# Sums of the first gate and up blocks in the banks of the products, and a scheduler that counts VectorE's work on SBUF as longer beside GpSimd

## The chip, the cores and the metric

The kernel runs on one core of one Trainium2 chip. The metric is the device time of one execution in microseconds, the median of several runs. The engines are called PE (TensorE, matrix products), PEld (its weight loads), DVE (VectorE), ACT (ScalarE), POOL (GpSimd) and SP (SyncE, which issues transfers here). Matrix products write to banks of PSUM, of which this part of the kernel uses eight; everything else on the chip lies in SBUF.

## The reference

One layer of a streaming encoder over 1056 tokens (1024 of a prompt and 32 of a running stream), with D_MODEL = 1024 and D_FF = 2816:

```python
def merge_and_tail(x, o_a, o_r, gate_a, gate_r, p, w_o, g_ffn, w_ff_gate, w_ff_up,
                   w_ff_down, g_ple, w_ple, w_ple_gate):
    mix = jax.nn.sigmoid(gate_a) * o_a + jax.nn.sigmoid(gate_r) * o_r
    x = x + mix @ w_o
    h = rmsnorm(x, g_ffn)
    x = x + (jax.nn.silu(h @ w_ff_gate) * (h @ w_ff_up)) @ w_ff_down
    gate = jax.nn.sigmoid(rmsnorm(x, g_ple) @ w_ple_gate)
    return x + gate * (p @ w_ple)
```

Ahead of it stand a projection of the normed input, an attention with two softmax maps per head and a retention. All inputs are float32, and every product is made of three float16 products (high by high, high by low, low by high parts).

## The kernel before

The kernel has four stages: projection, attention and retention (to 1085 us of the trace); the product with `w_o`, the residual and the norm; the gate and up products of 22 blocks of 128 columns; the down product and the tail. The change touches the second and third, which one hand-written scheduler (class `Flow`) orders together.

**Scheduler.** Work is written as generators that yield what they need: `V(n)`, `S(n)`, `G(n)` and `M(us)` are dictionaries from an engine to a cost in microseconds, `either(...)` offers one operation to two engines, `("get", key)` and `("put", key)` take and give back one of a kind of buffer, `("wait", key)` waits for an event. `Flow.run` keeps a clock per engine. Again and again it takes the candidate with the smallest key, writes it out, and so fixes the order of each engine's instructions. The key of a step with one possible engine is its start, `max(ready, engine free)`; the key of a step that two engines could take is its start plus 0.3 times its cost there. At equal keys the priority decides. On the chip each engine then works through its instructions in this order and waits at each for its inputs; the counted times play no part there.

**The second stage.** The tokens are cut in four pieces c0 to c3 (352, 352, 176 and 176 wide). `stream_bc` makes eight products with `w_o` of each piece. `residual(c)` adds each to the residual (L1534), squares and sums (L1542 on ACT, L1545 on DVE), sums over partitions with four small products (L1553), computes the root (L1557 on DVE, a power on POOL at L1560), spreads it (L1563 on DVE, a product at L1568) and scales the eight rows (L1572). The sums over partitions and the spread root lie in one PSUM bank, `ss`, allocated once as `ssb`.

**Seven products instead of eight.** The gate and up products use a Strassen-like scheme with seven products A1, S1, A2, S2, A4, S4, S3 of combined inputs x1, t1, x3, t2, t4, x4, t3. `sums(c, k)` builds t1 to t4 and x4 of an odd piece from it and the piece before, for k from 0 to 3; each addition and subtraction goes through `either_tt` (L1480), so DVE or POOL makes it. `parts16` splits each result in its high part (ACT, L1488) and its low part (through `either_tt`, L1482). The parts of x1, x3, t1 and x4 lie in the tile `mixs`, those of t2, t3 and t4 in `tT0` for the pieces c0 and c1 (352 wide) and `tT1` for c2 and c3 (176 wide). `gu_pair(j, p)` makes the seven products of block j for the pair p of pieces, in the order above, each into one of seven banks `ps`; the order of the pairs is (0,0), (1,0), (0,1), (1,1), (2,0), (2,1), (3,0) and so on. A product has 12 matrix multiplications, three for each k.

**The weights of a block.** `load_gu(j)` loads them (tile `st`), squares and sums on ACT (L1611), adds two partial sums (DVE, `wamh`, L1615), sums over partitions with one small product in `weight_scale` (PE, L300), makes the power of two from it (DVE, `p2of` and on, `guc` at L230 first), forms four combinations on POOL (`comb_w`, L1591) and splits seven times (ACT L1583, DVE L1586). The product of L300 writes into column 511 of `ssb`, the bank that the norm uses too, whose last readers are the scalings of L1572.

`gu_sums` then adds the products up out of the banks (ACT L1721, DVE L1715 and L1730), and `gu_out` makes the gated output (L1686 to L1695).

Of the kernel before, what the change touches and what calls it, by code (L numbers as in the profile page):

```python
# [21 lines left out]
P = 128  # L22
# [37 lines left out]
    return {"V": 0.07 + x + f * n / 960.0}  # L60


def S(n, x=0.0):
    return {"S": 0.1 + x + n / 1200.0}

# [11 lines left out]


def either(*ds):
    out = {}  # L80
    for d in ds:
        out.update(d)
    return out


class Flow:
# [65 lines left out]
    def run(self):  # L152
        while self.ready:
            best = None
            for c in self.ready:
                for e, us in c[4].items():
                    start = max(c[3], self.free[e])
                    k = (start + 0.0 if len(c[4]) == 1 else start + 0.3 * us, c[1], c[2])
                    if best is None or k < best[0]:
                        best = (k, c, e, start, us)  # L160
            _, c, e, start, us = best
            self.ready.remove(c)
            self.free[e] = start + us
            c[3] = start + us + (0.0 if e == "M" else LAT)
            self._step(c, e)
        assert not self.sleepers and not any(self.waiting.values())
# [17 lines left out]
def kernel(  # L184
# [104 lines left out]
    def weight_scale(amax, n, gi, tag, pool=True, norm=False, total=False, at_bank=None):  # L289


        p2 = sm(n, tag + "p2", 3)
        if total:
            if at_bank is None:
                yield ("wait", "id")
            key, psum = at_bank or ("o", ps_o)
            yield ("get", key)
            yield M(0.06)
            ps = psum[:, 511:512] if at_bank else psum.tile([P, 512], F32, tag=key, name="mt")[:, 0:1]
            nc.tensor.matmul(out=ps, lhsT=ones16, rhs=amax, start=True, stop=True)  # L300
            yield ("delay", 0.3 if at_bank else 0.0)
            yield from p2of(p2, ps, n, tag, norm)
            yield ("put", key)
        elif pool:
            yield G(0, 0.1)
            ar = sm(n, tag + "ar", 3)
            nc.gpsimd.partition_all_reduce(ar, amax, P, ABSMAX)
            yield from p2of(p2, ar, n, tag)
        else:
            ar = yield from spread_max(amax, n, tag, at_bank)  # L310
            yield from p2of(p2, ar, n, tag, norm)
            yield ("put", at_bank[0] if at_bank else "o")
        yield V(n)
        s = sm(n, tag + "s", 3)
        nc.vector.reciprocal(s, p2)
        yield V(n, 2.0)
        nc.vector.tensor_scalar(out=s, in0=s, scalar1=_f(2.0 ** (-52 if gi == 1 else -50)) if norm else 16384.0,
                                scalar2=None, op0=ALU.mult)
        d = sm(n, tag + "d", 6)
        if gi is None:  # L320
            nc.vector.tensor_scalar(out=d, in0=p2, scalar1=_f(2.0 ** (50 if norm else -14)), scalar2=None, op0=ALU.mult)
        else:
            nc.vector.tensor_scalar(out=d, in0=p2, scalar1=gd[:, gi:gi + 1], scalar2=_f(2.0 ** 64) if norm else 1.0,
                                    op0=ALU.mult, op1=ALU.mult)
        return s, d
# [1117 lines left out]
    with ExitStack() as pc:  # L1443
# [18 lines left out]
        with ExitStack() as pw:  # L1462
# [6 lines left out]

            mixs = xh1 = tail["mixs"]  # L1470
            xfs, gus, dns, banks, done = [], {}, {}, {}, []
            ssb = pss.tile([P, 512], F32, tag="ss", name="ss")

            def span(c):
                return slice(START[c], START[c] + WIDTH[c])
# [2 lines left out]
                return psb.tile([P, 512], F32, tag="ps", name="ps")[:, 0:WIDTH[c]]  # L1478

            def either_tt(n, out, in0, in1, op):  # L1480
                g = yield either(V(n), G(n))
                ENG[g].tensor_tensor(out=out, in0=in0, in1=in1, op=op)  # L1482


# [36 lines left out]
            def residual(c):  # L1521

                p, odd = divmod(c, 2)
                CW = WIDTH[c]
                cs = span(c)
                xf = xc.tile([P, KD, CW], F32, tag="xf%d" % p, name="xf", bufs=2)
                nc.sync.dma_start(out=xf, in_=xT[:, :, cs])
                xfs.append(xf)
                yield ("get", "acc")
                acc = wkb.tile([P, CH], F32, tag="acc", name="acc")[:, 0:CW]  # L1530
                for m in range(KD):
                    yield ("wait", ("wo", c, m))
                    yield V(CW, 1.0, 0.08)
                    nc.vector.scalar_tensor_tensor(out=xf[:, m], in0=banks[c, m], scalar=wos[m // 4][1][m % 4 // 2], in1=xf[:, m],  # L1534
                                                   op0=ALU.mult, op1=ALU.add)
                    yield ("put", "ps")
                    nc.sync.dma_start(out=x1_d[m, :, cs], in_=xf[:, m])
                    if m:
                        yield ("get", "sq")
                    yield S(CW, 0.05)  # L1540
                    sq = wkb.tile([P, CH], F32, tag="sq", name="sq")[:, 0:CW] if m else acc
                    nc.scalar.activation(sq, xf[:, m], AF.Square)  # L1542
                    if m:
                        yield V(CW)
                        nc.vector.tensor_tensor(out=acc, in0=acc, in1=sq, op=ALU.add)  # L1545
                        yield ("put", "sq")
                yield ("get", "ss")
                yield ("delay", 2.0 if c + 1 < NW else 0.5)
                yield M(0.3)
                B = CW // 4  # L1550
                ps = ssb
                for b in range(4):
                    nc.tensor.matmul(out=ps[0:B, CW + b:CW + b + 1], lhsT=acc[:, b * B:(b + 1) * B], rhs=ones32[:, 0:1],  # L1553
                                     start=True, stop=True)
                yield V(4, 1.0, 0.1)
                v = sm(4, "nbv")
                nc.vector.tensor_scalar(out=v[0:B], in0=ps[0:B, CW:CW + 4], scalar1=_f(1.0 / D), scalar2=EPS, op0=ALU.mult, op1=ALU.add)  # L1557
                yield G(4, 0.2)
                r = sm(4, "nbr")
                nc.gpsimd.tensor_tensor(out=r[0:B], in0=v[0:B], in1=neghalf[0:B], op=ALU.pow)  # L1560
                yield V(CW)
                dg = wkb.tile([P, CH], F32, tag="dg", name="dg")[:, 0:CW]
                nc.vector.tensor_tensor(out=dg[0:B].rearrange("p (b c) -> p b c", b=4),  # L1563
                                        in0=id32[0:B, 0:B].unsqueeze(1).broadcast_to([B, 4, B]),
                                        in1=r[0:B].unsqueeze(2).broadcast_to([B, 4, B]), op=ALU.mult)
                yield ("delay", 2.0 if c + 1 < NW else 0.5)
                yield M(0.5)
                nc.tensor.matmul(out=ps[:, 0:CW], lhsT=ones32[0:B], rhs=dg[0:B], start=True, stop=True)  # L1568
                yield ("put", "acc")
                for k in (0, 4, 1, 5, 2, 6, 3, 7):  # L1570
                    yield V(CW, 1.0, 0.08)
                    nc.vector.scalar_tensor_tensor(out=xf[:, k], in0=xf[:, k], scalar=gS[:, 1, k:k + 1], in1=ps[:, 0:CW],  # L1572
                                                   op0=ALU.mult, op1=ALU.mult)
                    if not odd:
                        flow.add(parts16((p, "x1" if k < HK else "x3", k % HK), (xh1[:, k, 0, cs], xh1[:, k, 1, cs]), xf[:, k]))
                    elif k >= HK:
                        flow.add(sums(c, k - HK))
                yield ("put", "ss")


            def split(j, w, s, i, src):
                yield S(HK * P, 0.18)
                nc.scalar.activation(w[:, i, 0], src, AF.Copy, scale=s)  # L1583
                yield ("delay", 0.4)
                yield V(HK * P, 1.0, 0.06)
                nc.vector.scalar_tensor_tensor(out=w[:, i, 1], in0=src, scalar=s, in1=w[:, i, 0], op0=ALU.mult, op1=ALU.subtract)  # L1586
                yield ("set", ("gw", j, i))

# [5 lines left out]
            def load_gu(j):  # L1594
# [19 lines left out]
                am = sm(1, "wamh", 3, BF16)  # L1614
                nc.vector.tensor_tensor(out=am, in0=am2[:, 0:1], in1=am2[:, 1:2], op=ALU.add)  # L1615
                yield ("delay", 1.5)
                s, d = yield from weight_scale(am, 1, 1, "gu", norm=True, total=True, at_bank=("sw", ssb))

                yield V(1, 1.0, 0.2)
                nc.vector.tensor_scalar(out=rf[:, j:j + 1], in0=d, scalar1=_f(2.0 ** 38), scalar2=d, op0=ALU.mult, op1=ALU.mult)  # L1620
# [21 lines left out]
            def load_dn(m):  # L1642
# [22 lines left out]
                yield V(2)  # L1665
                am = sm(1, "wamh", 3, BF16)
                nc.vector.tensor_tensor(out=am, in0=ams[:, 0:1], in1=ams[:, 1:2], op=ALU.add)
                s, d = yield from weight_scale(am, 1, None, "dn", norm=True, total=True, at_bank=("sw", ssb))
                for st, js in sts:
                    yield S(half * P, 0.18)  # L1670
                    nc.scalar.activation(w[:, 0, js], st, AF.Copy, scale=s)
# [155 lines left out]
                                halves[m, c] = bank()  # L1827
                            down_mm(halves[m, c], dns[m][0], js, c, js[0] < 16, False)

            flow = Flow(dict(ps=7, ss=1, sw=1, w=3, st=2, pr=2, th=2, acc=2, sq=2))  # L1830
            del flow.buffers["w"][1:], flow.buffers["st"][1:]
            with tc.manual_schedule(engines={mybir.EngineType.PE, mybir.EngineType.DVE, mybir.EngineType.Activation,
                                             mybir.EngineType.Pool}):
# [207 lines left out]
```

## Time and profile before

| | |
|---|---|
| median of 3 runs | 1947.84 us (1945.46 to 1948.18) |
| the profiled execution | 1947.6 us, its span 1945.8 us |
| granted clock of PE, mean | 0.994 of full |
| HBM, read and written | 113.61 MB and 31.34 MB, 74 GB/s over the span |

The table's second row is the time that the steps below are set against: the span and 1.8 us around it. The views used are the busy time by stretch, PE's waits, the instructions in order of time, and the groups by line. A bracket at the end of a row of the timeline tells how long the engine sat idle ahead of it and what ended that. A record's length contains some overlap with the next one, since instructions of an engine are pipelined; from start to start is the pace.

### The profile page before, as it was taken

The numbers are of one execution on the slowest core, as the hardware profiler recorded it, in microseconds if no ns is written. First come the engines' busy times: TensorE is split into PE (matmuls) and PEld (weight loads), VectorE is DVE, ScalarE is ACT, GpSimd is POOL, SyncE is SP. The second block draws the span as 40 slices with busy tenths as digits, with TensorE's granted clock in tenths as the row PEclk, the third lists the DMA queues.
The fourth block names the chain that finished last, engine by engine and source line by source line (L and its number), as shares of the span: only waits on it lengthen the run. The fifth ranks groups of instructions, "written<-read, shape, count | busy, mean of one in ns | idle before, by whom it ended". The sixth has DMA issues, their size and how long they took to land.

```text
span 1945.8 us, 38415 instructions
## 1 busy us (share of the span) xinstructions
PE 1885.6 (97%) x14267; PEld 1216.2 (63%) x14267; DVE 1531.5 (79%) x3995; ACT 1065.3 (55%) x2775; POOL 697.0 (36%) x1142
## 2 busy tenths in 40 slices
PE   5899999999999999999999998899999999999999
PEld 2465565555655555556556685777777776666665
DVE  7887878788878788878888579999999986753364
ACT  6676767666666666666665346555555552111132
POOL 3754444344454444444543048323223210000010
PEclk9899999999999999999999999999999999999999
DMA  5221202112121121120213721122211107211031
GB/s 194 72 72 53 83 20 72 56 49 63 33 76 59 28 79 41 52 81 18 75 57 127 268 71 34 72 94 81 74 66 45 66 31 261 78 60 61 28 131 49
DMA packets 71949, 147.44 MB, mean 76 GB/s; under 512 B 25265, under 2 KB 52017, under 8 KB 63825
## 3 DMA queue, kind: packets, MB, share of 16 engines
q1 hardware_dynamic: 71760, 144.98, 22.3%
q8 instruction: 112, 1.84, 0.4%
q14 instruction: 77, 0.62, 0.1%
HBM read 113.61 MB, written 31.34 MB: 74 GB/s over the span
## 4 chain that ended last, share of the span: by engine, by line
PE 83%; DVE 10%; ACT 2%; POOL 2%; issue 2%; DMA 1%; SPq 0%; DVEq 0%; POOLq 0%; ACTq 0%
PE pj L723 10%; PE pj L725 9%; PE pj L724 9%; PE ps L471 9%; PE ps L473 9%; PE ps L472 9%; PE ps L1458 4%; PE ps L1456 4%; PE ps L1457 4%; PE t L907 2%; PE sc L860 2%; PE sc L863 1%; PE pj L734 1%; PE t L1055 1%; PE po L926 1%
## 5 line engine op out<-in xcount | busy, mean ns | idle before, releaser
L723 PE MATMUL pj<-w,xh 128*128 128x512 f16 x1024 | 390.6, 381 | 0.7 <-ACT w L462 0.7
L724 PE MATMUL pj<-w,xh 128*128 128x512 f16 x1024 | 389.8, 381 | 1.4 <-DVE w L464 1.4
L725 PE MATMUL pj<-w,xh 128*128 128x512 f16 x1024 | 389.8, 381 | 0.0
L471 PE MATMUL ps<-mixs,w 128*128 128x352 f16 (+1 forms) x960 | 260.6, 277 | 1.5 <-DVE pws L1336 1.5
L472 PE MATMUL ps<-mixs,w 128*128 128x352 f16 (+1 forms) x960 | 260.5, 276 | 0.3 <-POOL mixs L1482 0.3
L473 PE MATMUL ps<-mixs,w 128*128 128x352 f16 (+1 forms) x960 | 260.4, 276 | 0.0
L471 PEld LDWEIGHTS <-w 128*128 128x128 f16 x1728 | 169.7, 98 | 65.6 <-issue 7.0
L473 PEld LDWEIGHTS <-w 128*128 128x128 f16 x1728 | 169.4, 98 | 55.1 <-issue 4.2
L472 PEld LDWEIGHTS <-w 128*128 128x128 f16 x1728 | 169.5, 98 | 49.6 <-issue 0.8
L725 PEld LDWEIGHTS <-xh 128*128 128x128 f16 x1024 | 100.5, 98 | 124.3 <-DVE xh L708 2.5
L1591 POOL TENSOR_TENSOR st<-st 128x512 f32<-128x512 f32 x66 | 85.9, 1301 | 251.5 <-DVE w L1586 187.0
L723 PEld LDWEIGHTS <-xh 128*128 128x128 f16 x1024 | 101.3, 99 | 77.5 <-issue 1.1
L878 ACT ACTIVATE p<-sc,nb,scs 128x256 f32<-128x256 f32 (+7 forms) x128 | 106.1, 830 | 77.6 <-DVE nb L872 29.9
L472 PE MATMUL ps<-tT,w 128*128 128x352 f16 (+1 forms) x528 | 143.6, 277 | 3.6 <-DVE tT L1482 3.6
L724 PEld LDWEIGHTS <-xh 128*128 128x128 f16 x1024 | 100.5, 98 | 72.7 <-issue 0.8
L473 PE MATMUL ps<-tT,w 128*128 128x352 f16 (+1 forms) x528 | 143.7, 277 | 0.0
L471 PE MATMUL ps<-tT,w 128*128 128x352 f16 (+1 forms) x528 | 143.6, 277 | 0.0
L1586 DVE SCALAR_TENSOR_TENSOR w<-st,gus,w 128x512 f16<-128x512 f32 x132 | 140.4, 1064 | 0.1
L870 DVE TENSOR_REDUCE nm<-sc 128x1 f32<-128x768 f32 (+6 forms) x112 | 102.5, 916 | 27.0 <-PE sc L863 25.5
L1458 PE MATMUL ps<-a,w 128*128 128x352 f16 x312 | 97.5, 313 | 0.5 <-DVE w L1677 0.5
L1457 PE MATMUL ps<-a,w 128*128 128x352 f16 x312 | 97.5, 313 | 0.0
L1456 PE MATMUL ps<-a,w 128*128 128x352 f16 x312 | 97.5, 312 | 0.0
(433 smaller groups left out, 4890.0 us busy)
## 6 DMA issues: line engine op xcount, KB each, us to landing
st<-in_win_dram SPq DMA_DIRECT2D x30, 1024.0 KB, 4.9
st<-in_wgu_dram SPq DMA_DIRECT2D x22, 1024.0 KB, 4.9
st<-in_wdn_dram SPq DMA_DIRECT2D x16, 704.0 KB, 4.5
out_dram<-kv SPq DMA_DIRECT2D x64, 128.0 KB, 1.7
a_d<-a SPq DMA_DIRECT2D x9, 528.0 KB, 2.6
b<-a_d SPq DMA_DIRECT2D x9, 528.0 KB, 8.5
mixs<-mix_d SPq DMA_DIRECT2D x8, 528.0 KB, 6.2
pw_d<-pws SPq DMA_DIRECT2D x12, 352.0 KB, 5.6
```

Of the source, the lines that this page charges most:

```text
L471: nc.tensor.matmul(out=ps, lhsT=wh, rhs=ah, start=first, stop=False)
L472: nc.tensor.matmul(out=ps, lhsT=wh, rhs=al, start=False, stop=False)
L473: nc.tensor.matmul(out=ps, lhsT=wl, rhs=ah, start=False, stop=last)
L723: nc.tensor.matmul(out=ps, lhsT=xhi, rhs=w[:, k, 0], start=(k == 0), stop=False)
L724: nc.tensor.matmul(out=ps, lhsT=xhi, rhs=w[:, k, 1], start=False, stop=False)
L725: nc.tensor.matmul(out=ps, lhsT=xh[:, k, 1, t0:t0 + P], rhs=w[:, k, 0], start=False, stop=(k == KD - 1))
L870: nc.vector.tensor_reduce(out=nm[0:R, mc], in_=pv, axis=AX.X, op=ALU.max, negate=True)
L878: nc.scalar.activation(pt[0:R, 0:NK], ps[0:R, p0:p0 + NK], AF.Exp, bias=nb[0:R, m:m + 1], scale=sc_ap[0:R], accum_out=Z[0:R, m:m + 1])
L1456: nc.tensor.matmul(out=ps, lhsT=wt[:, 0, j], rhs=a[:, 0, cs], start=(first and j == js[0]), stop=False)
L1457: nc.tensor.matmul(out=ps, lhsT=wt[:, 1, j], rhs=a[:, 0, cs], start=False, stop=False)
L1458: nc.tensor.matmul(out=ps, lhsT=wt[:, 2, j], rhs=a[:, 1, cs], start=False, stop=(last and j == js[-1]))
L1586: nc.vector.scalar_tensor_tensor(out=w[:, i, 1], in0=src, scalar=s, in1=w[:, i, 0], op0=ALU.mult, op1=ALU.subtract)
```

## The change

Three things are altered. First, `V` work that lies in SBUF alone in these stages (the additions of `either_tt`, the sums of squares, the spread root, the splits) is marked as `Shared`, and the scheduler adds to its counted cost on DVE up to 0.9 of it, as far as POOL is still taken by the scheduler's own clock. Second, the sums of `weight_scale` get a bank of their own: for blocks 0 to 3 the next of the seven banks `ps`, for the later ones and the down blocks a new tile in the bank `ss`. Third, the norm takes a new tile of that bank for each piece, and the buffer kind `sw` is gone. What is computed is the same.

```diff
+class Shared(dict):
+    pass
+
+def VS(n, f=1.0, x=0.0):
+    return Shared(V(n, f, x))
...
 def either(*ds):
-    out = {}
+    out = type(ds[0])()
...
                 for e, us in c[4].items():
                     start = max(c[3], self.free[e])
+                    if e == "V" and isinstance(c[4], Shared):
+                        us += 0.9 * min(us, max(0.0, self.free["G"] - start))
                     k = (start + 0.0 if len(c[4]) == 1 else start + 0.3 * us, c[1], c[2])
...
-            ps = psum[:, 511:512] if at_bank else psum.tile([P, 512], F32, tag=key, name="mt")[:, 0:1]
+            ps = psum.tile([P, 512], F32, tag=key, name="mt")[:, 0:1]
             nc.tensor.matmul(out=ps, lhsT=ones16, rhs=amax, start=True, stop=True)
...
-            ssb = pss.tile([P, 512], F32, tag="ss", name="ss")
...
-                g = yield either(V(n), G(n))
+                g = yield either(VS(n), G(n))
...
-                        yield V(CW)
+                        yield VS(CW)
                         nc.vector.tensor_tensor(out=acc, in0=acc, in1=sq, op=ALU.add)
...
-                ps = ssb
+                ps = pss.tile([P, 512], F32, tag="ss", name="ss")
...
-                yield V(HK * P, 1.0, 0.06)
+                yield VS(HK * P, 1.0, 0.06)
...
-                s, d = yield from weight_scale(am, 1, 1, "gu", norm=True, total=True, at_bank=("sw", ssb))
+                s, d = yield from weight_scale(am, 1, 1, "gu", norm=True, total=True, at_bank=("ps", psb) if j < 4 else ("ss", pss))
...
-                s, d = yield from weight_scale(am, 1, None, "dn", norm=True, total=True, at_bank=("sw", ssb))
+                s, d = yield from weight_scale(am, 1, None, "dn", norm=True, total=True, at_bank=("ss", pss))
...
-            flow = Flow(dict(ps=7, ss=1, sw=1, w=3, st=2, pr=2, th=2, acc=2, sq=2))
+            flow = Flow(dict(ps=7, ss=1, w=3, st=2, pr=2, th=2, acc=2, sq=2))
```

The order of the instructions changes from the norm of c1 on, on all engines. Lines behind the edits stand nine further down (L1482 is L1491 in the new file, L1591 is L1600).

POOL's queue, before, where the low parts of the first pair end and the combinations of block 1 begin. `tT0_16839` takes low parts of t2, t3 and t4 of c0 and c1 (from `xf_16850`, the rows of c0, and `xf_16853`, those of c1), `w_17827` and `st_17103` belong to block 1:

```order
L1482 TENSOR_TENSOR tT0_16839<-xf_16850,tT0_16839 128x352
L1482 TENSOR_TENSOR mixs_16401<-xf_17104,mixs_16401 128x176 x2
L1482 TENSOR_TENSOR tT0_16839<-xf_16853,tT0_16839 128x352
L1482 TENSOR_TENSOR tT0_16839<-xf_16850,tT0_16839 128x352
L1591 TENSOR_TENSOR w_17827<-st_17103 128x512
L1560 TENSOR_TENSOR nbr_18093<-nbv_18090,neghalf_68 44x4
L1591 TENSOR_TENSOR st_17103<-st_17103 128x4x128 x3
```

The same queue now, where its last three low parts for `tT0_16839` stand. `st_17675` belongs to block 2, `xf_17103` and `xf_17416` are the rows of c2 and c3, `xf_16849` and `xf_16852` those of c0 and c1 (t4 of k = 2, t2 of k = 3 and t4 of k = 3, in this order):

```order
L1491 TENSOR_TENSOR xf_17103<-xf_17416,xf_17103 128x176
L1600 TENSOR_TENSOR st_17675<-st_17675 128x4x128
L1491 TENSOR_TENSOR tT1_16840<-xf_17103,tT1_16840 128x176
L1491 TENSOR_TENSOR tT1_16840<-xf_17416,tT1_16840 128x176
L1600 TENSOR_TENSOR st_17675<-st_17675 128x4x128
L1491 TENSOR_TENSOR mixs_16401<-xf_17103,mixs_16401 128x176
L1491 TENSOR_TENSOR tT1_16840<-xf_16849,tT1_16840 128x176
L1491 TENSOR_TENSOR mixs_16401<-xf_17416,mixs_16401 128x176
L1491 TENSOR_TENSOR tT0_16839<-xf_16849,tT0_16839 128x352
L1491 TENSOR_TENSOR tT0_16839<-xf_16852,tT0_16839 128x352
L1491 TENSOR_TENSOR tT0_16839<-xf_16849,tT0_16839 128x352
```

What moved: the last low parts of the first pair stood ahead of all combinations of block 1 (one of them on DVE); now three of them stand behind all four combinations of blocks 1 and 2 each, and behind most sums of the pieces c2 and c3.

PE's queue before, at the sum over partitions of c3 (L1553) and at the spread root of c3 (L1568). The rows on `mixs` and `tT_16839` are products of the pair (0,0):

```order
L473 LDWEIGHTS w
L473 MATMUL ps<-mixs,w 128x352
L1553 MATMUL ss<-cst_sb,acc 44x1 x4
L471 LDWEIGHTS w
L471 MATMUL ps<-mixs,w 128x352
```

```order
L473 LDWEIGHTS w
L473 MATMUL ps<-tT_16839,w 128x352
L1568 MATMUL ss<-dg,cst_sb 128x176
L471 LDWEIGHTS w
L471 MATMUL ps<-tT_16839,w 128x352
```

The same place now, with the sum of block 2 (L310, into a bank of its own) behind it:

```order
L482 MATMUL ps<-mixs,w 128x352
L483 LDWEIGHTS w
L483 MATMUL ps<-mixs,w 128x352
L1562 MATMUL ss<-cst_sb,acc 44x1 x4
L1577 MATMUL ss<-dg,cst_sb 128x176
L310 LDWEIGHTS cst_sb
L310 MATMUL mt<-wamh,cst_sb 128x1
L481 LDWEIGHTS w
L481 MATMUL ps<-tT_16839,w 128x352
```

What moved: before, the products A2 and S2 (24 matrix multiplications) stood between the two steps of the norm of c3; now nothing does, and S2 with t2 stands behind both and behind the sum of block 2. The sum of block 1, which stood ahead of the first product of the pair (0,0), stands behind it.

More of the change, by code (lines that the diff above doesn't have):

```diff
@@ L1560, in residual @@
                 nc.gpsimd.tensor_tensor(out=r[0:B], in0=v[0:B], in1=neghalf[0:B], op=ALU.pow)
-                yield V(CW)
+                yield VS(CW)
                 dg = wkb.tile([P, CH], F32, tag="dg", name="dg")[:, 0:CW]
```

## The prediction

> **What bounds the kernel now.** First the span, then busy time by stretch: the columns behind the length are busy us (with the number of instructions) of PE, PEld, DVE, ACT and POOL, then PE's granted clock, the DMA share and GB/s.
>
> ```profile
> span 1945.8 us, 38415 instructions
> 1158.00:1268.00 110.00, 93.77 (x858) 73.44 (x856) 108.14 (x224) 62.90 (x146) 67.53 (x69) 0.95 0.16 55
> 1268.00:1608.00 340.00, 340.00 (x3038) 262.51 (x3036) 326.23 (x732) 195.95 (x404) 90.32 (x66) 1.00 0.19 65
> ```
>
> From 1268 us PE never rests for 340 us: what this change does there can gain nothing, unless it takes a matrix multiplication away, and it takes none. Between 1158 and 1268 us PE is idle for 16 us while DVE is busy for 108.14 of 110. That is the place the change works on: the end of the norm, the sums of the last pieces and the weights of the first blocks, all on DVE and POOL. Next, PE's waits from 1085 to 1640 us (total, times, longest), and the rows of PE's timeline at them:
>
> ```profile
> PE ss L300 <- DVE xf L1572: 8.4, 2, 6.3
> PE ps L472 <- DVE tT L1482: 3.6, 1, 3.6
> PE ss L300 <- DVE wamh L1615: 3.3, 2, 2.4
> PE ss L1568 <- DVE dg L1563: 0.4, 1, 0.4
> ```
> ```profile
> 1184.06 0.16 PE L300 MATMUL ss<-wamh,cst_sb 128*128 128x1 bf16 x1 [6.31 <-DVE xf L1572]
> 1184.09 0.45 PE L471 MATMUL ps<-mixs,w 128*128 128x352 f16 x1
> ...
> 1191.30 0.31 PE L471 MATMUL ps<-tT,w 128*128 128x352 f16 x1
> 1191.45 0.31 PE L472 MATMUL ps<-tT,w 128*128 128x352 f16 x1
> ...
> 1195.33 0.31 PE L473 MATMUL ps<-tT,w 128*128 128x352 f16 x1
> 1197.75 0.16 PE L300 MATMUL ss<-wamh,cst_sb 128*128 128x1 bf16 x1 [2.11 <-DVE xf L1572]
> ...
> 1221.63 0.31 PE L472 MATMUL ps<-tT,w 128*128 128x176 f16 x1 [3.60 <-DVE tT L1482]
> ...
> 1232.91 0.16 PE L300 MATMUL ss<-wamh,cst_sb 128*128 128x1 bf16 x1 [2.39 <-DVE wamh L1615]
> ...
> 1267.61 0.16 PE L300 MATMUL ss<-wamh,cst_sb 128*128 128x1 bf16 x1 [0.94 <-DVE wamh L1615]
> ```
>
> So in the pair (0,0) PE waits for block sums (L300), twice because these write into the bank whose last reader, a scaling of the norm (L1572), isn't through; the products with t2 (the first `tT` rows, from 1191.30 us) start without a wait.
>
> **The change part by part.** *The banks.* With banks of their own, the sums of blocks 1 and 2 no longer wait for the scalings: of 6.31 and 2.11 us those parts can go that were due to the bank. What is late next is `wamh`, which stands in DVE's queue in the middle of the same scalings (by the profile it was made 3.3 us ahead of the product at 1184.06 us):
>
> ```profile
> 1180.63 0.14 DVE L1615 TENSOR_TENSOR wamh<-gam 128x1 bf16<-128x1 f32 x1
> ```
>
> So 1 to 4 us could be gained at the first, as far as PE then has nothing worse to wait for.
>
> *The order on POOL.* It has something worse. In POOL's new queue the last three low parts of the first pair, t4 of k = 2, t2 of k = 3 and t4 of k = 3, stand behind the four combinations of block 1, the four of block 2 and most sums of c2 and c3. PE's product S2 of the pair (0,0) takes t2, k = 3 included, and its second matrix multiplication of k = 3 reads that low part; everything else of PE is queued behind. The time R at which POOL has it done is therefore a floor for PE. POOL's groups from 1158.5 to 1221.5 us, before:
>
> ```profile
> L1482 POOL TENSOR_TENSOR xf<-xf 128x352 f32<-128x352 f32 x10 | 10.0, 1001 | 8.2 <-DVE xf L1572 5.5 <-DVE xf L1482 2.6
> L1591 POOL TENSOR_TENSOR st<-st 128x512 f32<-128x512 f32 x6 | 9.0, 1507 | 1.2 <-DVE w L1586 1.0
> L1482 POOL TENSOR_TENSOR xf<-xf 128x176 f32<-128x176 f32 x12 | 8.4, 718 | 1.7 <-DVE xf L1572 0.8 <-DVE gup L234 0.8
> L1482 POOL TENSOR_TENSOR mixs<-xf,mixs 128x352 f16<-128x352 f32 x7 | 7.3, 1051 | 0.5 <-ACT mixs L1488 0.5
> L1482 POOL TENSOR_TENSOR mixs<-xf,mixs 128x176 f16<-128x176 f32 x9 | 6.2, 687 | 0.3 <-ACT mixs L1488 0.3
> L1482 POOL TENSOR_TENSOR tT<-xf,tT 128x176 f16<-128x176 f32 x7 | 5.0, 712 | 0.0
> L1482 POOL TENSOR_TENSOR tT<-xf,tT 128x352 f16<-128x352 f32 x4 | 4.1, 1045 | 0.0
> L1560 POOL TENSOR_TENSOR nbr<-nbv,neghalf 44x4 f32<-44x4 f32 x2 | 2.7, 1370 | 2.2 <-DVE nbv L1557 2.2
> L1591 POOL TENSOR_TENSOR w<-st 128x512 f32<-128x512 f32 x2 | 2.7, 1362 | 0.0
> ```
>
> The 21 wide additions took 21.4 us, 1.02 each; the 28 narrow ones 19.6, 0.70 each; the eight combinations 11.7; the two powers 2.7. The first group's 8.2 us of idle holds the 5.5 ahead of the first row; behind that POOL waited for 2.7 + 1.2 + 1.7 + 0.5 + 0.3 + 2.2 = 8.6 us. In the new queue, from its first addition to t2's last low part, stand 27 wide and 20 narrow additions, the eight combinations and the two powers: 27 x 1.02 + 20 x 0.70 + 11.7 + 2.7 = 55.9 us. POOL starts as before, since the norm of c0 and c1 ahead of it stays:
>
> ```profile
> 1158.64 1.98 POOL L1482 TENSOR_TENSOR xf<-xf 128x352 f32<-128x352 f32 x2 [5.51 <-DVE xf L1572]
> ...
> 1161.91 0.93 POOL L1482 TENSOR_TENSOR xf<-xf 128x352 f32<-128x352 f32 x1
> 1162.80 0.86 POOL L1482 TENSOR_TENSOR mixs<-xf,mixs 128x352 f16<-128x352 f32 x1
> ```
>
> 1158.64 + 55.9 = 1214.5 us without any wait. With all 8.6 us of waits it is 1223. I take half, 4.3, as the queue still has the power behind DVE's `nbv` and the combinations of block 2 behind DVE's splits: **R = 1218.8 us**. The low bound is POOL undisturbed: 0.81 to 0.89 us from start to start of wide additions at 1162 us, some 0.8 of the mean above, 44.7 us in all, R = 1203.
>
> *What stands beside POOL.* DVE's share of the same additions falls from 15 wide ones to 8, so DVE gets ahead of POOL. An addition of DVE's took 0.51 us at a pace of 0.43 while POOL was still, and 1.23 beside it:
>
> ```profile
> 1174.60 1.23 DVE L1482 TENSOR_TENSOR xf<-xf 128x352 f32<-128x352 f32 x1
> 1175.76 0.32 DVE L1545 TENSOR_TENSOR acc<-acc,sq 128x176 f32<-128x176 f32 x1
> 1176.01 1.17 DVE L1482 TENSOR_TENSOR mixs<-xf,mixs 128x352 f16<-128x352 f32 x1
> ...
> 1177.41 0.50 DVE L1482 TENSOR_TENSOR tT<-xf,tT 128x352 f16<-128x352 f32 x1
> 1177.85 0.51 DVE L1482 TENSOR_TENSOR xf<-xf 128x352 f32<-128x352 f32 x1
> ```
>
> The scheduler's new surcharge follows this, but moving a wide addition from DVE to POOL replaces 0.43 us of work by 0.81; it doesn't shorten the sum of the two. The Trainium skill, "SBUF — State Buffer", section "SBUF: two separate sides", says that DVE and GpSimd hold their shared pair of ports as an exclusive lock for a whole instruction, the loser blocking fully. The 0.51 beside 1.23 us agrees. By that rule the two engines' undisturbed times add up, and R would lie near 1223 rather than 1218.8, the time some 4 us higher; it speaks against a gain from this part.
>
> *The norm of c3.* Its partition sum and the spread root's product now stand one behind the other on PE, where A2 and S2 stood between. PE will wait there for `nbv`, the power and `dg`:
>
> ```profile
> 1189.60 0.15 DVE L1557 TENSOR_SCALAR nbv<-ss 44x4 f32<-44x4 f32 x1
> ...
> 1191.32 1.41 DVE L1563 TENSOR_TENSOR dg<-cst_sb,nbr 44x176 f32<-44x176 f32 x1 [0.91 <-POOL nbr L1560]
> ```
>
> Undisturbed this chain is 1189.60 to 1192.7, 3 us, and up to 8 where each of its steps queues behind others. It costs nothing, because the wait for R lies behind it and covers it; were t2's part early, it would cost these 3 to 8.
>
> *The sum.* From R, PE has two more matrix multiplications of S2 and the twelve of A4: 14 at 0.149 us (1191.30 to 1191.45). After the 6.31 us gap 24 of them, 3.58 us at that pace, took from 1184.09 to the partition sums at 1189.07 us, the clock being lower: 1.4 us more, which I add after this longer gap too:
>
> ```profile
> 1189.07 0.49 PE L1553 MATMUL ss<-cst_sb,acc 128*44 128x1 f32 x8
> ```
>
> A4 ends at 1218.8 + 2.1 + 1.4 = 1222.3 us; before it ended at 1195.33 + 0.31 = 1195.64. Loss 26.7 us. During that wait DVE and ACT finish what PE later waited for: the sums of c2 and c3 and the splits of blocks 1 and 2. So the gaps behind 1195.64 us go: 2.11, 3.60, 2.39, 0.94 and two short ones of 0.3 together, 9.4 us, and with the 3.60 us gap its slow start, another 1.4: 10.8. Net 26.7 - 10.8 = +15.9 us on the execution's 1947.6: **1963.5 us**. That execution lies 0.2 us under the median of 1947.84.
>
> The sums of the later blocks stand one product earlier in PE's queue. I cost this at nothing, since DVE's queue now has `wamh` ahead of the sums that it used to follow.
>
> **The rivals.** *Faster.* The low part is on time, and PE's last wait is the sum of block 2, at 1197.75 us as now. Then S2 and A4 follow, 24 x 0.149 + 1.4, A4 ends at 1202.7: 7.1 later, 10.8 gained, 1943.9 us. It needs R below 1198, that is POOL's 57 operations in 39 us, less than the undisturbed pace gives; it decides for "faster" at all from R = 1202.9 (1195.64 + 10.8 - 3.5). For it speaks only that DVE does fewer additions beside POOL. Chance 0.08.
>
> *The same.* The change spares contention: POOL runs at its undisturbed pace, R = 1203, and the loss of 10.9 equals the gain of 10.8: 1948 us. Against it: in this stretch DVE still has the splits, scalings, sums of squares and 30 additions. This case also takes in that the waits don't come as read. Chance 0.07.
>
> *Slower still.* The earlier place of the later blocks' sums does cost: one product is 12 x 0.149 = 1.79 us, and if `wamh` is late for 1.0 of it in each of some 18 later blocks, 18 us come on top, 1981. It decides where `wamh` ends less than 1.79 us ahead of L300 now. Against it: from 1268 us on PE has no idle time at all, and DVE's order moves along. Chance 0.05.
>
> **How the numbers follow.** The forecast, R between 1208 and 1226, has 0.80. R = 1208.3 gives 1953, R = 1226.3 gives 1971; R = 1203 to 1208, and a sum of a later block that waits for 2 or 3 us, fall to the remainders, so the range is 1953 to 1971 and leaves out about 0.2. A measurement of this kernel can tell some 0.2%, 3.9 us, from no change. Faster 0.08, same 0.07, slower 0.85.
>
> **What would show it.** Right: in PE's timeline one gap of over 15 us, ended by POOL's `tT` addition at about 1218 us, ahead of a `tT` product 352 wide, the next rows of PE's waits being a spread root of 3 to 8 us and block sums of 1 to 4; no gap over 1 us from there to 1270. Wrong: that gap under 5 us (POOL's queue is faster than its rows), or gaps at each block from 1300 us on, or new gaps behind A4 of the kind that I let vanish.

## The result and the profile after

The changed kernel took 1975.69 us in the median of 4 runs (1973.17 to 1977.15), the kernel before 1946.65 us in 4 (1945.27 to 1948.18). The ratio is 1.0145, 95% interval 1.013 to 1.016: 29 us slower. The forecast was slower by 15.9 us, 1963.5 us in a range of 1953 to 1971: the direction came true, the size did not.

The span, and the busy time of the two stretches that were shown of before, now of the changed kernel (the same columns):

```profile
span 1974.3 us, 38410 instructions
...
1158.00:1268.00 110.00, 79.25 (x730) 61.87 (x728) 93.80 (x184) 53.19 (x125) 64.39 (x66) 0.84 0.12 40
1268.00:1608.00 340.00, 328.10 (x2912) 251.30 (x2910) 323.39 (x716) 193.74 (x400) 93.47 (x70) 1.00 0.19 66
```

Two losses can be read there. In the first stretch PE is idle for 31 us where it was idle for 16. In the second it is idle for 12 us where it never rested. PE's waits from 1085 to 1640 us tell the two apart:

```profile
PE ps L482 <- POOL tT L1491: 19.3, 1, 19.3
PE mt L310 <- DVE wamh L1624: 15.7, 18, 2.3
PE ss L1577 <- DVE dg L1572: 6.8, 1, 6.8
```

The first row is the wait for the low part of t2; the second counts 18 waits for `wamh`, of which two lie ahead of 1200 us and sixteen behind 1280. In PE's timeline, with two of those sixteen:

```profile
1179.35 0.16 PE L310 MATMUL mt<-wamh,cst_sb 128*128 128x1 bf16 x1 [1.48 <-DVE wamh L1624]
...
1191.08 0.95 PE L1577 MATMUL ss<-dg,cst_sb 44*128 44x176 f32 x2 [6.76 <-DVE dg L1572]
...
1194.36 0.16 PE L310 MATMUL mt<-wamh,cst_sb 128*128 128x1 bf16 x1 [2.33 <-DVE wamh L1624]
...
1217.07 0.45 PE L482 MATMUL ps<-tT,w 128*128 128x352 f16 x1 [19.30 <-POOL tT L1491]
1217.32 0.50 PE L483 MATMUL ps<-tT,w 128*128 128x352 f16 x1
1217.61 0.50 PE L481 MATMUL ps<-tT,w 128*128 128x352 f16 x1
...
1221.13 0.50 PE L481 MATMUL ps<-mixs,w 128*128 128x352 f16 x1
...
1222.79 0.31 PE L481 MATMUL ps<-mixs,w 128*128 128x352 f16 x1
...
1282.88 0.24 PE L481 MATMUL ps<-mixs,w 128*128 128x176 f16 x1
...
1417.52 0.16 PE L310 MATMUL mt<-wamh,cst_sb 128*128 128x1 bf16 x1 [0.71 <-DVE wamh L1624]
...
1436.30 0.31 PE L483 MATMUL ps<-tT,w 128*128 128x352 f16 x1
1437.31 0.16 PE L310 MATMUL mt<-wamh,cst_sb 128*128 128x1 bf16 x1 [0.71 <-DVE wamh L1624]
```

S4, the first product behind A4, starts at 1221.13 us where it started at 1197.77 (with the sum of block 2 just ahead of it): 23.4 us later. The row at 1282.88 us is the first of a block's narrow products (176 wide). The same row stood at 1267.64 before, so 15.2 us of the 23.4 are left: the gaps that lay between are gone. The rest of the loss comes behind it. A wait shown as 0.71 us costs more than that: from start to start it is 1436.30 to 1437.31, 1.01 us where 0.15 is the pace, so 0.86; a record overlaps the next one by the difference. From sum to sum a block now takes 1417.52 to 1437.31, 19.79 us, and took 18.92 before:

```profile
1400.09 0.17 PE L300 MATMUL ss<-wamh,cst_sb 128*128 128x1 bf16 x1
...
1419.01 0.17 PE L300 MATMUL ss<-wamh,cst_sb 128*128 128x1 bf16 x1
```

The sixteen waits hold 15.7 - 1.48 - 2.33 = 11.9 us of idle time and 16 x 0.15 us of overlap, 14.3 us. One of them (0.47 us) lies ahead of the row at 1282.88, and one wait of 0.5 us of before, at the start of the down product, is gone. 15.2 + 14.3 - 0.6 - 0.6 = 28.3 us; the spans differ by 28.5.

POOL's groups from 1158.5 to 1217.2 us, the stretch of which the forecast had made its sum:

```profile
L1491 POOL TENSOR_TENSOR tT<-xf,tT 128x352 f16<-128x352 f32 x11 | 11.9, 1088 | 0.0
L1491 POOL TENSOR_TENSOR xf<-xf 128x352 f32<-128x352 f32 x11 | 11.2, 1025 | 0.1
L1491 POOL TENSOR_TENSOR xf<-xf 128x176 f32<-128x176 f32 x11 | 8.6, 809 | 0.6 <-DVE xf L1581 0.3 <-DVE xf L1491 0.3
L1600 POOL TENSOR_TENSOR st<-st 128x512 f32<-128x512 f32 x6 | 8.2, 1364 | 0.0
L1491 POOL TENSOR_TENSOR mixs<-xf,mixs 128x352 f16<-128x352 f32 x5 | 4.6, 911 | 0.5 <-ACT mixs L1497 0.5
L1491 POOL TENSOR_TENSOR mixs<-xf,mixs 128x176 f16<-128x176 f32 x5 | 3.8, 758 | 2.1 <-ACT mixs L1497 2.1
L1600 POOL TENSOR_TENSOR w<-st 128x512 f32<-128x512 f32 x2 | 2.7, 1358 | 0.0
L1569 POOL TENSOR_TENSOR nbr<-nbv,neghalf 44x4 f32<-44x4 f32 x2 | 2.7, 1336 | 1.6 <-DVE nbv L1566 1.6
L1491 POOL TENSOR_TENSOR tT<-xf,tT 128x176 f16<-128x176 f32 x4 | 2.4, 612 | 0.0
```

27 wide additions took 27.7 us, 1.03 each; 20 narrow ones 14.8, 0.74 each; the combinations 10.9, the powers 2.7: 56.1 us, and 4.9 us of waits. That is 61.0 us by the lengths of the records, a little more than the 59.6 us that passed, since POOL's records overlap too (one of 0.93 us in the prediction's rows takes 0.89 from start to start).

### The profile page after: what moved, and what is told of

It reads as the page before. It is cut to its first block, busy times and chain, and to the rows that moved or that the text cites. A ratio compares the mean times of both kernels' runs of the same rounds, so it can differ in the third digit from the quotient of the medians.

```text
span 1974.3 us, 38410 instructions
## 1 busy us (share of the span) xinstructions
PE 1888.8 (96%) x14267; PEld 1215.4 (62%) x14267; DVE 1537.7 (78%) x3994; ACT 1065.6 (54%) x2775; POOL 698.1 (35%) x1143
## 4 chain that ended last, share of the span: by engine, by line
PE 75%; DVE 15%; ACT 4%; POOL 3%; issue 2%; DMA 1%; SPq 0%; DVEq 0%; POOLq 0%; ACTq 0%
PE pj L733 9%; PE pj L735 9%; PE pj L734 9%; PE ps L481 6%; PE ps L482 6%; PE ps L483 6%; PE ps L1467 4%; PE ps L1466 4%; PE ps L1468 4%; DVE w L1595 4%; PE t L917 2%; PE sc L870 2%; PE sc L873 1%; PE pj L744 1%; PE t L1065 1%
## 5 line engine op out<-in xcount | busy, mean ns | idle before, releaser
L1600 POOL TENSOR_TENSOR st<-st 128x512 f32<-128x512 f32 x66 | 86.9, 1316 | 222.2 <-DVE w L1595 115.5
L482 PE MATMUL ps<-tT,w 128*128 128x352 f16 (+1 forms) x528 | 144.6, 279 | 19.3 <-POOL tT L1491 19.3
L1595 DVE SCALAR_TENSOR_TENSOR w<-st,gus,w 128x512 f16<-128x512 f32 x132 | 122.8, 933 | 1.3 <-ACT w L1592 1.2
L1592 ACT ACTIVATE w<-st,gus 128x512 f16<-128x512 f32 x132 | 90.1, 713 | 55.1 <-DVE gus L327 46.3
L1467 PE MATMUL ps<-a,w 128*128 128x352 f16 x312 | 97.6, 313 | 0.0
L1466 PE MATMUL ps<-a,w 128*128 128x352 f16 x312 | 97.6, 313 | 0.0
```

The source lines that it names most:

```text
L482: nc.tensor.matmul(out=ps, lhsT=wh, rhs=al, start=False, stop=False)
L1466: nc.tensor.matmul(out=ps, lhsT=wt[:, 0, j], rhs=a[:, 0, cs], start=(first and j == js[0]), stop=False)
L1467: nc.tensor.matmul(out=ps, lhsT=wt[:, 1, j], rhs=a[:, 0, cs], start=False, stop=False)
```

## The experiments

Each time is a median, each ratio one to the kernel before on the same chip.

**The two parts apart.** First the banks alone, the counting plain:

```diff
 def VS(n, f=1.0, x=0.0):
-    return Shared(V(n, f, x))
+    return V(n, f, x)
```

> Only the banks are changed, the counting is plain, and every engine's order is that of before. Theory (the order made the loss, the banks only free a wait): the gap ahead of the sum of block 1, 6.31 us before, shrinks to 1 to 4 us and the 2.11 us one to under 1; as DVE is nearly always busy there, part of it comes back in the 3.60 us gap; the time is 1 to 5 us under before. No waits of block sums from 1300 us on. Rival (sums in banks of the products starve the products): 5 us or more over before.

Measured: 1947.1 us, ratio 0.9995 (0.9986 to 1.0004). The two gaps shrank about as thought, but little of that reached the time: the median is 1.6 us under that of the kernel before (1948.73 us on this chip), inside the expected 1 to 5, and the interval holds 1. PE's timeline of this run:

```profile
1180.31 0.16 PE L310 MATMUL mt<-wamh,cst_sb 128*128 128x1 bf16 x1 [3.07 <-DVE wamh L1624]
...
1187.43 0.46 PE L1562 MATMUL ss<-cst_sb,acc 128*44 128x1 f32 x8 [1.98 <-DVE gus L325]
...
1195.65 0.16 PE L310 MATMUL mt<-wamh,cst_sb 128*128 128x1 bf16 x1 [1.02 <-DVE wamh L1624]
...
1215.45 0.24 PE L482 MATMUL ps<-mixs,w 128*128 128x176 f16 x1 [1.83 <-POOL mixs L1491]
...
1220.92 0.31 PE L482 MATMUL ps<-tT,w 128*128 128x176 f16 x1 [3.49 <-DVE tT L1491]
```

6.31 us became 3.07 and 2.11 became 1.02; in their place stand 1.98 us ahead of the partition sums of c3, and 1.83 us where 0.34 was. All waits but one are for DVE, which is busy for 108.15 of the 110 us from 1158 to 1268 us. So most of a wait taken away there came back at DVE's next late result.

Then the counting alone, in the new code with the old bank:

```diff
...
-                ps = pss.tile([P, 512], F32, tag="ss", name="ss")
+                ps = ssb
...
-                s, d = yield from weight_scale(am, 1, 1, "gu", norm=True, total=True, at_bank=("ps", psb) if j < 4 else ("ss", pss))
+                s, d = yield from weight_scale(am, 1, 1, "gu", norm=True, total=True, at_bank=("sw", ssb))
...
```

> Only the counting is changed, the sums stay in the norm's bank. Theory: the order is that of after, so the 19 us gap on POOL's low part and the 0.7 us waits at each later block stay; 1972 to 1980 us. Rival (the banks have a part in the loss): under 1968 us.

Measured: 1978.27 us, ratio 1.0153 (1.0139 to 1.0166). PE waits 15.8 us for POOL's low part (not 19, as two sums now wait 9.0 us ahead of it for scalings in the shared bank) and 16 times for `wamh`, 11.9 us in all. So the counting alone, that is the new order, makes a loss of this size, and the banks are not needed for it.

**The two losses apart.** The later blocks' sums counted 0.5 us later. POOL's order is that of the changed kernel to the last row; the order on DVE and ACT moves along with the sums in the later blocks:

```diff
-                yield ("delay", 1.5)
+                yield ("delay", 1.5 if j < 4 else 2.0)
                 s, d = yield from weight_scale(am, 1, 1, "gu", norm=True, total=True, at_bank=("ps", psb) if j < 4 else ("ss", pss))
```

> After, with the delay ahead of the sum of the blocks from 4 on counted as 2.0 us in place of 1.5: POOL's order is the same, the later sums stand three products later on PE. Theory (two separate losses): the 18 waits of 0.4 to 1.5 us for wamh from 1281 us on go, the 19 us gap stays, 1962 to 1966 us. Rival (DVE and ACT are the bound there and PE waits for them in any order): as much idle time at other places, 1972 us or more.

Measured: 1962.13 us, ratio 1.0074 (1.0061 to 1.0088): 13.6 us less than the changed kernel. The 19.3 us wait stays to the digit, and of the sixteen waits one of 0.48 us is left, beside the two ahead of 1200 us. PE's waits in this run:

```profile
PE ps L482 <- POOL tT L1491: 19.3, 1, 19.3
...
PE mt L310 <- DVE wamh L1624: 4.3, 3, 2.3
```

The low parts of t2 and t4 of the first pair without the 0.3 of their cost in the key:

```diff
+class Early(Shared):
+    pass
...
-                    k = (start + 0.0 if len(c[4]) == 1 else start + 0.3 * us, c[1], c[2])
+                    k = (start + 0.0 if len(c[4]) == 1 or isinstance(c[4], Early) else start + 0.3 * us, c[1], c[2])
...
-                g = yield either(VS(n), G(n))
+                g = yield (Early if early else Shared)(either(VS(n), G(n)))
...
-                yield from either_tt(CW, out[1], src, out[0], ALU.subtract)
+                yield from either_tt(CW, out[1], src, out[0], ALU.subtract, key[:2] in ((0, "t2"), (0, "t4")))
```

> After, with the low parts of t2 and t4 of the first pair taken without the surcharge for wide steps, so that POOL makes them ahead of the combinations of block 2. Theory: the 19.3 us gap ahead of S2 goes to under 8 us, the waits for dg and wamh ahead of it stay or grow by 1 to 4, the later 0.7 us waits stay: 1957 to 1966 us. Rival (the work of DVE and POOL on SBUF adds up, so what is made earlier makes other parts late by as much): the gap comes back at later products, 1970 us or more.

Measured: 1958.84 us, ratio 1.0053 (1.0039 to 1.0067): 16.9 us less than the changed kernel. The 19.3 us wait is gone, three of some 4 us stand in its place, and the later waits stay. PE's waits in this run:

```profile
PE mt L314 <- DVE wamh L1628: 12.3, 17, 1.5
PE ss L1581 <- DVE dg L1576: 4.1, 1, 4.1
PE ps L486 <- POOL tT L1495: 3.7, 1, 3.7
PE ps L486 <- POOL mixs L1495: 3.5, 1, 3.5
```

Both edits, the later sums and the early low parts, in one kernel:

> After, with both: the low parts of t2 and t4 of the first pair early on POOL, and the later blocks' sums counted 0.5 us later. Theory (two separate losses that add up): 1975.7 less 16.9 and less 13.6, 1945 us, 1943 to 1948; PE idles ahead of 1250 us at the same three places as with the early parts alone, 11 us in all, and from 1250 us on under 1 us. Rival (the gains overlap): 1953 us or more.

Measured: 1944.41 us, ratio 0.9983 (0.9974 to 0.9992). The two gains add up, 16.9 + 13.6 = 30.5 us expected and 31.3 found, so the losses are two and apart. PE idles for 11.3 us from 1160 to 1250 us, at the three places said, and for 0.97 us from there to 1640. With both losses out of it, the changed kernel is 0.17% faster than before.

That kernel still waits 4.1 us for `dg`. With the spread root of c3 counted later, so that work stands ahead of it:

```diff
-                yield ("delay", 2.0 if c + 1 < NW else 0.5)
+                yield ("delay", 2.0 if c + 1 < NW else 4.0)
                 yield M(0.5)
```

> As the run with both, with the delay ahead of the spread root of c3 counted as 4.0 us in place of 0.5, so that two products and the sum of block 2 stand between the partition sums and the spread root. Theory (PE's 4.1 us wait for dg there is the cost of having nothing between): that wait goes under 1 us, but the scalings behind it come 2 to 3 us later, so 1 to 3 us are gained, 1941 to 1946 us. Rival (DVE and POOL bind in that stretch, so the wait moves to the narrow products): within 1 us of the run with both.

Measured: 1952.38 us, ratio 1.0018 (1.0009 to 1.0027), 8 us more: neither theory. The wait for `dg` went, and larger ones came: two of 6.6 and 2.6 us for narrow low parts of POOL's, beside the 3.5 us that was there already. The scalings of c3 began at 1200.34 us where they had begun at 1196.04, and all that is made of them came later. PE's waits in this run:

```profile
PE ps L486 <- POOL mixs L1495: 12.6, 3, 6.6
```

**Why the later sums wait.** In the changed kernel a later block's sum stands behind the fifth wide product of a block (from block 7 on), in the kernel before behind the seventh. The place alone, put on the kernel with the banks alone:

```diff
-                yield ("delay", 1.5)
+                yield ("delay", 1.5 if j < 4 else 1.0)
                 s, d = yield from weight_scale(am, 1, 1, "gu", norm=True, total=True, at_bank=("ps", psb) if j < 4 else ("ss", pss))
```

> The banks alone, in plain counting, with the delay ahead of the sum of the blocks from 4 on counted as 1.0 us in place of 1.5: the sums of the later blocks stand on PE where they stand in after, POOL's order is that of before. Theory (the place on PE alone makes the later waits): some 16 waits of 0.7 us for wamh from 1290 us on, each 0.86 us from start to start, and 1959 to 1962 us. Rival (the counting moved work on DVE and ACT and so made wamh late): no such waits, 1945 to 1950 us.

Measured: 1949.23 us, ratio 1.0005 (0.9996 to 1.0014): the rival. The sums stand where they stand in the changed kernel, and from 1290 us on none waits. So the place is not the cause by itself, and by the run with the later sums neither is the new counting: it takes the earlier place and the order that the counting makes on DVE and ACT. Selected rows of ACT, DVE and PE in one block of this run, from the last narrow product ahead of the sum on:

```profile
1408.77 0.24 PE L483 MATMUL ps<-tT,w 128*128 128x176 f16 x1
...
1413.92 0.33 DVE L1699 SCALAR_TENSOR_TENSOR th<-th,snq 128x176 f32<-128x176 f32 x1
...
1414.03 0.60 ACT L1702 ACTIVATE a<-th 128x176 f16<-128x176 f32 x2 [1.22 <-DVE th L1699]
...
1414.87 1.06 ACT L1620 ACTIVATE w<-st 128x1024 bf16<-128x1024 f32 x1
...
1416.25 1.07 ACT L1620 ACTIVATE w<-st 128x1024 bf16<-128x1024 f32 x1
...
1417.44 0.16 DVE L1624 TENSOR_TENSOR wamh<-gam 128x1 bf16<-128x1 f32 x1 [1.60 <-ACT w L1620]
...
1417.80 0.17 PE L310 MATMUL mt<-wamh,cst_sb 128*128 128x1 bf16 x1
```

And in the changed kernel:

```profile
1427.42 0.24 PE L483 MATMUL ps<-tT,w 128*128 128x176 f16 x1
...
1433.91 0.35 ACT L1702 ACTIVATE a<-th 128x176 f16<-128x176 f32 x1 [0.72 <-DVE th L1699]
1434.17 1.04 ACT L1620 ACTIVATE w<-st 128x1024 bf16<-128x1024 f32 x1
...
1434.96 0.33 DVE L1699 SCALAR_TENSOR_TENSOR th<-th,snq 128x176 f32<-128x176 f32 x1
...
1435.33 0.35 ACT L1702 ACTIVATE a<-th 128x176 f16<-128x176 f32 x1
...
1435.92 1.06 ACT L1620 ACTIVATE w<-st 128x1024 bf16<-128x1024 f32 x1
...
1437.10 0.16 DVE L1624 TENSOR_TENSOR wamh<-gam 128x1 bf16<-128x1 f32 x1 [0.18 <-ACT w L1620]
```

From the last narrow product's start, PE comes to the sum after 9.03 us in both (1417.80 - 1408.77; 1436.30 + 0.15 - 1427.42). `wamh` ends 8.83 us after it in the run and 9.84 in the changed kernel, where ACT's second square (L1620) starts at 8.50 us against 7.48. Ahead of it in ACT's queue stand two `a` (L1702) of the narrow output, in the changed kernel one ahead of the first square and one behind it, in the run both ahead of it, and each needs a `th` of DVE's (L1699). The first starts at 6.49 us against 5.26, and ACT sits idle ahead of it. The second `th` runs at 7.54 us against 5.15, behind a split and an `a` of DVE's (L1704); the second `a` follows 0.04 us after its end, just as ACT is through with the first square. So the new order on DVE and ACT makes `wamh` 1.0 us later, and this place leaves 0.2 us of room. That it is these two rows of that order rather than others is read from the rows, and wasn't tried by itself.

**Which of the counts.** The splits alone counted plainly:

```diff
-                yield VS(HK * P, 1.0, 0.06)
+                yield V(HK * P, 1.0, 0.06)
```

> After, with the splits alone counted plainly as before. POOL's queue still has a low part of the first pair behind the combinations of block 2; the later blocks' sums stand on PE, and their squares on ACT, as before. Theory (the surcharge on the additions makes the late low part, that on the splits the later waits): a gap of 10 us or more ended by a low part stays, no wamh wait over 0.3 us from 1300 us on, 1955 to 1965 us. Rival (the additions' surcharge makes both): the 0.7 us waits stay, 1970 us or more.

Measured: 1963.61 us, ratio 1.0081 (1.0067 to 1.0095). One gap of 20.4 us in S2 stays, ended by a low part on DVE this time, and the wait for the spread root of c3 ahead of it is 9.3 us (6.8 in the changed kernel). No sum of a block waits longer than 0.22 us. So the first loss comes without the surcharge on the splits: the one on the additions, the sums of squares and the spread root is enough.

The other way round, the splits alone with the surcharge (the additions, the sums of squares and the spread root plainly):

```diff
-                g = yield either(VS(n), G(n))
+                g = yield either(V(n), G(n))
...
-                        yield VS(CW)
+                        yield V(CW)
                         nc.vector.tensor_tensor(out=acc, in0=acc, in1=sq, op=ALU.add)
...
-                yield VS(CW)
+                yield V(CW)
                 dg = wkb.tile([P, CH], F32, tag="dg", name="dg")[:, 0:CW]
```

> After, with the splits alone counted with the surcharge, and the additions, the sums of squares and the spread root plainly. POOL takes the low parts of the first pair ahead of the combinations, as before. Theory: no gap over 5 us in the pair (0,0), and since the later blocks' sums stand as before here, no later waits: 1945 to 1951 us. Rival (the surcharge on the splits is enough for a loss): 1957 us or more.

Measured: 1942.97 us, ratio 0.9973 (0.9964 to 0.9983), the fastest of all, 2 us under the expected range's lower end. No later sum waits for over 0.5 us from 1290 us on, so the splits' surcharge alone doesn't make the second loss, and the theory of the run above is wrong there: it takes both. PE's waits from 1160 to 1700 us add up to 12.1 us against 16.6 before. The 3.60 us that before waited for a narrow low part of DVE's are 0.26 here. What in the order brought that wasn't tried, and by the intervals this run can't be told from the one with both edits. PE's timeline of this run:

```profile
1215.42 0.24 PE L482 MATMUL ps<-tT,w 128*128 128x176 f16 x1 [0.26 <-DVE tT L1491]
```

Last, the early low parts (the edit shown above) with the splits counted plainly:

> After, with the low parts of t2 and t4 of the first pair early and the splits counted plainly. Theory (both losses gone, each in another way than by the delay): 1942 to 1947 us, no wamh wait over 0.6 us from 1260 us on. Rival (the later waits return in another form, or a narrow low part is late instead): 1950 us or more.

Measured: 1946.78 us, ratio 0.9995 (0.9986 to 1.0004): no large loss, and no gain either. No sum waits from 1260 us on.

## Why the prediction was right in direction and wrong in size

- *Where the change can act.* "What this change does there can gain nothing" held for the stretch behind 1268 us, but a loss was possible there, and about half of the loss fell there.
- *The banks.* "1 to 4 us could be gained at the first" held for that gap (6.31 to 3.07 us), while the time can't be told from before's (ratio 0.9995): DVE binds there.
- *R.* Right. POOL started at 1157.46 us and S2 went on at 1217.07: 59.6 us, against 1218.8 - 1158.64 = 60.2. The pieces fit as well: 56.1 us of work (55.9 said) and 4.9 of waits (4.3 said, half of those of before, which was a choice and came out by luck). That POOL starts as before did not hold: it started 1.2 us earlier. From the exclusive lock in the Trainium skill ("SBUF — State Buffer", section "SBUF: two separate sides") the prediction drew that R would lie near 1223, 64.4 us after POOL's start; the trace stays 4.8 us under that. But 1223 was POOL's queue with all of its old waits, not a sum over both engines, so no run here tests the rule by it.
- *What lies ahead of it.* Right: 6.8 us for the spread root (3 to 8 said), 1.48 and 2.33 us for the sums (1 to 4), covered by the wait for R: in the run with both edits, where that cover is gone, 4.1 us for the spread root remained and the time was still under before.
- *The clock.* Mis-sized: from R to S4 it took 1221.13 - 1217.07 = 4.06 us, 3.5 said, and S4 still began slowly. The 20 matrix multiplications up to 1222.79 us took 5.72 us, and 20 x 0.149 is 2.98: 2.7 us lost to the clock, 1.4 said.
- *The gaps that go.* Right: no gap from 1217 to 1268 us. Up to 1282.88 us the kernel had lost 15.2 us, or 16.4 from POOL's start, of 15.9 said. That this is so close is luck in part, since POOL's earlier start and the clock's 1.3 us offset each other.
- *The later blocks.* This step failed: "The sums of the later blocks stand one product earlier in PE's queue. I cost this at nothing, since DVE's queue now has `wamh` ahead of the sums that it used to follow." They cost 14.3 us. Only the first two of them stand one product earlier; from block 7 on it is two; and the prediction followed DVE's queue to `wamh` and no further, one step short: `wamh` needs ACT's two squares, and those stand behind outputs that need DVE. The mechanism stood among the rivals, at 18 us and a chance of 0.05, with its own test: whether `wamh` ends less than 1.79 us ahead of the sum. The trace of before answers it:

```profile
1418.22 0.15 DVE L1615 TENSOR_TENSOR wamh<-gam 128x1 bf16<-128x1 f32 x1
```

It ends 0.64 us ahead of the sum at 1419.01 us (shown above). The prediction's own sign of being wrong, gaps at each block from 1300 us on, is what the trace shows. The row above asked for a far larger chance, though not for certainty, as the run with the place alone shows. That PE had no idle time there, the argument against this rival, told nothing of the room ahead of the sum. 15.9 and 14.3 together are 30 us; 29 were measured.

## What to carry to other kernels

A penalty in a scheduler's key that grows with a step's cost can let many cheap steps pass a dear one, here until PE waited 19 us for it: look up which step the next engine needs first, and where it stands in the queue, before any sum of costs. Where a wait moves forward in a loop's steady state, follow what it needs through every engine back to the loop's own output; 0.86 us per turn cost nearly as much here as one wait of 19 us. And put a change of counts in place one kind of step at a time: here one of the kinds alone gave 0.27%, and all together lost 1.45%.

## What the runs showed of the hardware

After the 19.3 us wait matrix multiplications came every 0.29 us in place of 0.15 (1217.32 to 1217.61 in PE's timeline above) until 1222.79 us, and then at the full pace from one to the next. The row of the six microseconds behind the wait has a granted clock of 0.53 (the number behind POOL's busy time):

```profile
1217.00:1223.00 6.00, 5.93 (x22) 3.05 (x22) 5.05 (x11) 1.65 (x5) 2.00 (x4) 0.53 0.50 175
```

After the 0.7 us waits of the later blocks there was nothing of the kind: the stretch from 1268 to 1608 us, which holds them, has a granted clock of 1.00. And a wide addition of DVE's could cost far more beside POOL than the 1.23 us that before showed. In the changed kernel one took 3.75 us (0.51 with POOL idle), while POOL beside it began wide additions at 1174.88, 1175.98, 1176.87 and 1177.68 us, at most 1.10 us apart:

```profile
1175.23 3.75 DVE L1491 TENSOR_TENSOR mixs<-xf,mixs 128x352 f16<-128x352 f32 x1
```
